# A hybrid encoder layer on one core: stores of transposed queries and keys on another DMA queue, in other slots, and the order of the loads ahead of the first attention head

## The chip, the core and the metric

The kernel runs on one core of a Trainium2 chip. The core has five engines with an instruction stream each: TensorE (PE in the profile; its weight loads are PEld), VectorE (DVE), ScalarE (ACT), GpSimd (POOL) and SyncE (SP). SyncE and ScalarE issue the DMAs of this kernel; in the profile their queues are SPq and ACTq. An engine works through its stream in order, and so does each queue's issuer: an issue that has to wait holds up what stands behind it. The metric is the time of one execution on the device in microseconds. The kernel before took 578.08 us, the median of three runs (575.47 to 578.79).

## What is computed

One layer of an encoder on 1024 tokens of width 1024, with 16 learned tokens ahead of them. The input is normalised once and projected into three groups of mixers: a gated short convolution (256 columns), multi-head attention with compressed queries and keys (8 heads of 64 + 32 features), and a retention mixer (4 heads of 64). The outputs are gated, put side by side and projected back.

```python
u = rms_norm(h, ln_w[l])
(cx, cb, cc, cz, cq, ckv, krope, mz, rq, rk, rv, rz) = jnp.split(u @ w_in[l], IN_OFFSETS, axis=-1)
y_conv = short_conv_mixer(cx, cb, cc, cz, conv_w[l], conv_b[l])
y_mla = mla_mixer(cq, ckv, krope, mz, ...)      # softmax(q k^T) v per head, under a chunk-causal mask
y_ret = retention_mixer(rq, rk, rv, rz, ...)    # intra-chunk scores plus a running state
h = h + jnp.concatenate([y_conv, y_mla, y_ret], axis=-1) @ w_out[l]
```

## The kernel before

Everything is kept in float32. A float32 operand of a matrix product is split into a high part (`h`, rounded by ScalarE) and a low part (`l`, the rest, subtracted by VectorE or GpSimd), and `mm3` (line 114) makes three products of the two pairs. The weights come in tiles of 128 rows by 512 columns (256 KB): SyncE loads one into a staging tile `ws` (three buffers), ScalarE casts its high half and VectorE or GpSimd subtracts its low half (`load_w`, line 117, and `split`, line 102). High and low tiles have 12 buffers each, so the tiles of the next unit of weights can be loaded only as those of the unit before are used up.

The stages follow each other on TensorE: the gates `mz`; the compressed queries and keys `A`, from which `a_up` makes keys and queries of all heads and stores them as `k_s` and `q_s` in DRAM, token by token (lines 392 and 412); the retention mixer in two units `u` of two heads, each over token tiles `t` (`r_proj`, `r_rope`, `r_score`, `r_out`); the convolution in two units and two halves of the tokens `g` (`conv_cx`, `conv_cz`, `conv_cb`, all through `feat`); the attention heads; the output projection `out`. The products of `r_proj` and of `feat` go to a pair of PSUM banks of tag `pj`; ScalarE frees one with `rt` (line 463), VectorE one with the convolution's products (lines 646 to 676).

The attention needs queries and keys with the features on the partitions. This is made beside the retention and convolution stages in eight turns, `turn(i, part)` (line 552): turn `i` treats the keys (`i` even) or the queries (`i` odd) of one pair of heads. Part 0 gathers them from DRAM into `ts` (four loads of 192 KB on SyncE), part 1 transposes them on VectorE into `td` (line 564), part 2 splits them into high halves `th` (ScalarE) and low parts (VectorE, in place in `td`), the queries by single features and with a scale, part 3 stores them in `T_s`, as `kT_s` or `qT_s` (two stores of 384 KB from `th`, one of 768 KB from `td`, lines 582 and 583). `turns()` (line 585) is called once for each token tile of the retention stage and once for each product group of the convolution; each call is a slot. A turn begins in the slot that `BEGIN` names; its part 1 comes two slots later, part 2 three, part 3 four. The tiles `ts` and `td` share two buffers (tag `q`), the halves `th` share two (tag `v`) with the values of the heads, of which `load_pair(0)` (line 686) loads the first behind the convolution's third group (slot 31); the fourth group has slots 32 to 35.

The program is written in this order, but each engine's final order is laid out ahead of the run by a scheduler that simulates the program and gives an engine the earliest written instruction that is ready in the simulation. `tc.issue_after(x)` keeps the instructions in its block that run on the engine of `x` behind `x`; `at["act"]` and `at["dve"]` are the last `rt`, `th` of the gate, or eviction noted. It has no effect on instructions of other engines.

Ahead of the attention, `load_wo` (line 689) loads a tile of output weights (256 KB, SyncE) and returns the splitting of it as a function, `cut`; `load_head(h)` (line 615) loads keys and queries of a head, six loads of 128 KB into `kt` and three of 256 KB into `qt`; `y_split` (line 844) loads finished outputs `y_s` of the other mixers for the `partial` products (line 853), which are spread over the attention as filling. `score(h, t)` (line 748) makes one tile of scores `S`, their maximum and exponentials.

Of the kernel before, what the change touches and what calls it, by code (L numbers as in the profile page):

```python
# [7 lines left out]
F32 = mybir.dt.float32  # L8
# [42 lines left out]
def trunk(tc, ins, outs):  # L51
    from contextlib import ExitStack

    nc = tc.nc
# [27 lines left out]
    T_s = [dp.tile([4, 2, P, 6, 256], F32, name=f"{c}T_s") for c in "qk"]  # L82
# [11 lines left out]
    r = cp.tile([P, 9], F32, name="r")  # L94
# [7 lines left out]
    def split(hi, lo, src, scale=None, lo_eng=None):  # L102

        if scale is None:
            nc.scalar.copy(hi, src)
            (lo_eng or nc.vector).tensor_tensor(lo, src, hi.bitcast(F32), op=ALU.subtract)
        else:
            nc.scalar.activation(hi, src, AF.Copy, scale=scale)
            nc.vector.scalar_tensor_tensor(lo, src, scale, hi.bitcast(F32), op0=ALU.mult, op1=ALU.subtract)
# [63 lines left out]
    with tc.tile_pool(name="ps0", bufs=1, space=PSUM, reuse_waits="tile") as ps0:  # L173
# [96 lines left out]
        for b in range(4):  # L270
# [3 lines left out]
            for g in range(2):  # L274
                i = 2 * b + g
# [47 lines left out]
    act = [None]  # L323
# [122 lines left out]
    oz, at = {}, {}  # L446
# [100 lines left out]
        later(fin)  # L547

    turned, slot = {}, [0]
    BEGIN = (2, 5, 8, 11, 17, 20, 23, 26)  # L550

    def turn(i, part):

        hp, which = i // 2, 1 - i % 2
        if part == 0:
            src = hp_pool.tile([P, NT, 192], F32, tag="q", name=f"ts{i}")
            x = (q_s, k_s)[which].rearrange("t p c -> (t p) c")[:, hp * 192:hp * 192 + 192]
            for j, y in enumerate(x.rearrange("(j n r) c -> j r n c", j=4, r=32)):
                nc.sync.dma_start(src[32 * j:32 * j + 32], y)
            turned[i] = [src]  # L560
        elif part == 1:
            dst = hp_pool.tile([P, 6, 256], F32, tag="q", name=f"td{i}")
            for j in range(2):
                nc.vector.transpose(dst[:, 3 * j:3 * j + 3].rearrange("p c (n k) -> p n c k", k=32),
                                    turned[i][0][:, :, 96 * j:96 * j + 96].rearrange("p n (c k) -> p n c k", k=32))
            turned[i] = [dst]
        elif part == 2:
            dst = turned[i][0]
            for j in range(2):
                hi = hp_pool.tile([P, 3, 256], F32R, tag="v", name=f"th{i}_{j}")  # L570
                x = dst[:, 3 * j:3 * j + 3]
                if which:
                    split(hi, x.bitcast(F32R), x)
                else:

                    for c in range(3):
                        split(hi[:, c], x[:, c].bitcast(F32R), x[:, c], scale=wqk[:, c:c + 1] if c < 2 else None)
                turned[i].append(hi)
        else:
            dst, *hi = turned.pop(i)  # L580
            for j in range(2):
                nc.sync.dma_start(T_s[which][hp, 0, :, 3 * j:3 * j + 3], hi[j].bitcast(F32))
            nc.sync.dma_start(T_s[which][hp, 1], dst)

    def turns():

        n = slot[0]
        slot[0] += 1
        for ago, part in ((4, 3), (3, 2), (2, 1), (0, 0)):
            if n - ago in BEGIN:  # L590
                with tc.issue_after(at["act" if part == 2 else "dve"]):
                    turn(BEGIN.index(n - ago), part)

    for u in range(2):
        for t in [8] + list(range(NT)):
            r_proj(u, t)
            step()
            if t != 8:
                turns()
            if t == 3:  # L600
                if u == 0:
                    wr.append([load_w("r1", k) for k in range(KT)])
                else:
                    wc = [[load_w("c0", k) for k in range(KT)]]


    def feat(u, b, lo_, n, name):
        pp = pst("pj", name)
        for k in range(KT):
            mm3(pp[:, :n], [w[:, b * P:b * P + P] for w in wc[u][k]], X(k, lo_, n), k == 0, k == KT - 1)  # L610
        step()
        turns()
        return pp

    def load_head(h):
        for which in (1, 0):

            src = T_s[which][h // 2].rearrange("s (i f) c r -> c f (s i) r", i=4)
            x = ((qT, kT)[which][h % 2])[:, :, NM * which:NM * which + SEQ].bitcast(F32)
            for c in range(3):  # L620
                cs, y = slice(32 * c, 32 * c + 32), src[3 * (h % 2) + c]
                if which:
                    for s in range(2):
                        nc.sync.dma_start(x[cs, s].rearrange("p (i r) -> p i r", i=4), y[:, 4 * s:4 * s + 4])
                else:
                    nc.sync.dma_start(x[cs].rearrange("p s (i r) -> p (s i) r", i=4), y)
        for i, m_ in enumerate((kmh, kml)):
            nc.gpsimd.tensor_copy(kT[h % 2][:96, i, :NM], m_[:, h].bitcast(F32))

# [59 lines left out]
    def load_wo(k, g):  # L689
        wh = wp.tile([P, 512], F32R, tag="wh", name=f"woh{k}_{g}")  # L690
        wl = wp.tile([P, 512], F32R, tag="wl", name=f"wol{k}_{g}")
        st = at1.tile([P, 512], F32, tag="wst", name=f"wos{k}_{g}", bufs=4)
        nc.sync.dma_start(st, wout_d[:, k, g * 512:g * 512 + 512])
        wo[k, g] = (wh, wl)

        def cut():
            split(wh, wl, st, scale=vec[:, V_RN:V_RN + 1] if k >= 6 else None, lo_eng=nc.gpsimd if g == 0 else nc.vector)
        return cut
# [46 lines left out]
    if True:  # L745
# [98 lines left out]
        def y_split(t):  # L844
            src = wsp.tile([P, 512], F32, tag="ws", name=f"ysrc{t}")
            nc.sync.dma_start(src.rearrange("p (k q) -> p k q", k=4), y_s.rearrange("k p q -> p k q")[:, :, t * P:t * P + P])
            return lambda: y_cut(t, src)
# [16 lines left out]
        seq = [(h, t) for h in range(H) for t in range(NT)]  # L864


    cuts = [load_wo(k, 0) for k in (0, 1, 6, 7)]
    load_head(0)
    ycuts = [y_split(t) for t in range(2)]
    load_head(1)  # L870
    conv_cx(1, 1, 1)
    conv_cx(1, 1, 0)
# [27 lines left out]
    for n in range(len(seq) + 1):  # L900
        if n + LA < len(seq):
            score(*seq[n + LA])
        if n < len(seq):
            h, t = seq[n]
            p_t(h, t)
            turns()
            if t == 0 and h in (0, 2, 4):
                pairs.append(load_pair(h // 2 + 1))
                nc.sync.dma_start(ym[h // 2 + 1], mz_s[h // 2 + 1])

            if t == QK and h + 2 < H:
                load_head(h + 2)
        if 1 <= n and seq[n - 1][1] % 4 == 3:
            attend(seq[n - 1][0], seq[n - 1][1] // 4)
        if n < len(seq):
            h, t = seq[n]
# [146 lines left out]
```

## Time and profile before

| | |
|---|---|
| median of the runs | 578.08 us (575.47 to 578.79, three runs) |
| the profiled execution | 578.73 us, its span 576.6 us |
| TensorE busy | 565.5 us (98%) |
| VectorE, ScalarE, GpSimd busy | 357.9, 253.8, 212.3 us |
| mean granted TensorE clock | 0.993 of full speed |
| SyncE's queue, ScalarE's queue | 84.39 MB, 6.29 MB |

The span goes from the first to the last instruction of one execution. The granted clock is given as a share of 2.4 GHz, 0.5 being 1.2 GHz. In the views below, a wait is put down to the instruction whose end came last before it; a DMA share of 1 or more in a stretch means that the 16 DMA engines had no free time.

### The profile page before, as it was taken

The page shows a single profiled execution, that of the slowest core. Times are in us where ns is not written, and L with a number is a line of the kernel's source. Part 1 is how long each engine was busy: PE and PEld are TensorE (multiplying, and loading weights), DVE is VectorE, ACT ScalarE, POOL GpSimd, SP SyncE. Part 2 cuts the span into 40 slices and gives each one's busy share as a digit, 9 for nine tenths or more (in the row PEclk, how much of TensorE's full clock was granted, in tenths as well). Part 3 has the DMA queues.
Part 4 walks back from the last instruction along what each step waited for, and adds up shares of the span by engine and source line. Part 5 has one row for each costly group of instructions (what it writes and reads, how often), then busy time and mean ns, then how long its engine had stood idle before and what let it go on. Part 6 is the DMA issues. An engine that isn't in the chain of part 4 may idle for free.

```text
span 576.6 us, 9524 instructions
## 1 busy us (share of the span) xinstructions
PE 565.5 (98%) x3294; PEld 474.7 (82%) x3294; DVE 357.9 (62%) x782; ACT 253.8 (44%) x598; POOL 212.3 (37%) x314
## 2 busy tenths in 40 slices
PE   9999999999999999989999989999999999999997
PEld 5888999988887888888889878788788888877886
DVE  6958569887456654767375535766656755766132
ACT  7923465683244424534132114655545644654000
POOL 2123357767113140242231836454524424540000
PEclk9999999999999999989999989999999999999999
DMA  8563325374133634366557698845645637123086
GB/s 325 164 197 126 130 91 175 148 225 152 70 105 134 175 110 152 79 233 202 164 171 236 154 207 274 206 107 151 165 131 143 174 101 203 40 75 107 0 300 229
DMA packets 61567, 91.28 MB, mean 158 GB/s; under 512 B 5424, under 2 KB 35760, under 8 KB 61392
## 3 DMA queue, kind: packets, MB, share of 16 engines
q1 hardware_dynamic: 57920, 84.39, 49.4%
q10 hardware_dynamic: 3600, 6.29, 3.0%
q8 instruction: 26, 0.43, 0.3%
q14 instruction: 21, 0.17, 0.1%
HBM read 57.07 MB, written 33.59 MB: 157 GB/s over the span
## 4 chain that ended last, share of the span: by engine, by line
PE 85%; DVE 5%; DMA 4%; ACT 2%; issue 1%; POOL 1%; SPq 1%; DVEq 0%; POOLq 0%; ACTq 0%
PE r L114 13%; PE S L114 9%; PE mz L114 8%; PE out L114 8%; PE part L114 8%; PE A L114 7%; PE o L832 6%; PE pTp L791 5%; PE cv L114 5%; PE qps L114 3%; PE cz L114 3%; PE cb L114 2%; DMA ws_c<-in_win 2%; DMA ysrc<-y_s 1%; PE kps L114 1%
## 5 line engine op out<-in xcount | busy, mean ns | idle before, releaser
L114 PE MATMUL S<-kt,qt 104*128 104x144 f32 (+6 forms) x336 | 65.6, 328 | 1.6 <-DMA ysrc<-y_s 1.6
L769 ACT ACTIVATE pr<-S,smx 128x144 f32<-128x144 f32 (+8 forms) x72 | 50.3, 699 | 36.3 <-DVE smx L760 22.2
L760 DVE TENSOR_REDUCE smx<-S 128x1 f32<-128x144 f32 (+8 forms) x72 | 50.8, 705 | 20.7 <-PE S L114 9.3
L114 PEld LDWEIGHTS S<-kt,qt 104*128 104x128 f32 x336 | 54.9, 190 | 7.7 <-issue 2.3
L777 POOL TENSOR_SCALAR pm<-pr,smx 128x16 f32<-128x16 f32 x64 | 19.5, 304 | 85.8 <-DVE smx L775 80.8
L797 ACT COPY pt<-pTp 128x512 f32<-128x512 f32 (+2 forms) x64 | 32.2, 504 | 38.9 <-PE pTp L791 38.8
L778 POOL TENSOR_SCALAR pr<-pr,smx 128x128 f32<-128x128 f32 (+3 forms) x64 | 47.7, 746 | 0.0
L791 PE MATMUL pTp<-ident,pr 128*128 128x128 f32 x288 | 45.6, 277 | 1.3 <-DVE pt L795 0.9
L791 PEld LDWEIGHTS pTp<-ident,pr 128*128 128x128 f32 x288 | 34.2, 140 | 9.8 <-issue 3.7
L476 POOL TENSOR_SCALAR kw<-qk,con 128x64 f32<-128x64 f32 (+1 forms) x36 | 15.1, 433 | 70.2 <-DVE qk L472 58.6
L832 PE MATMUL o<-pt,v 128*64 128x256 f32 (+2 forms) x448 | 39.4, 311 | 0.0
L832 PEld LDWEIGHTS o<-pt,v 128*64 128x64 f32 x448 | 27.3, 136 | 11.2 <-issue 4.2
L114 PE MATMUL r<-wh_r,xah 128*128 128x512 f32 (+1 forms) x80 | 30.6, 382 | 0.0
L114 PE MATMUL r<-wl_r,xah 128*128 128x512 f32 (+1 forms) x80 | 30.2, 378 | 0.0
L951 DVE SCALAR_TENSOR_TENSOR ot<-out,xr 128x512 f32<-128x512 f32 (+1 forms) x17 | 11.2, 661 | 30.5 <-PE out L114 17.2
L114 PE MATMUL r<-wh_r,xal 128*128 128x512 f32 (+1 forms) x80 | 29.9, 373 | 0.0
L114 PE MATMUL part<-woh,yh 128*128 128x512 f32 x64 | 29.6, 463 | 0.0
L114 PE MATMUL r<-wl_r,xbh 128*128 128x512 f32 x64 | 26.0, 406 | 0.0
L114 PE MATMUL r<-wh_r,xbl 128*128 128x512 f32 x64 | 25.6, 400 | 0.0
L114 PE MATMUL r<-wh_r,xbh 128*128 128x512 f32 x64 | 25.6, 400 | 0.0
L114 PE MATMUL part<-wol,yh 128*128 128x512 f32 x64 | 25.3, 395 | 0.0
L114 PE MATMUL part<-woh,yl 128*128 128x512 f32 x64 | 25.1, 393 | 0.0
(276 smaller groups left out, 1558.0 us busy)
## 6 DMA issues: line engine op xcount, KB each, us to landing
kt<-kT_s SPq DMA_DIRECT2D x48, 128.0 KB, 4.2
qt<-qT_s SPq DMA_DIRECT2D x24, 256.0 KB, 5.8
ws_r<-in_win SPq DMA_DIRECT2D x16, 256.0 KB, 3.0
ws_c<-in_win SPq DMA_DIRECT2D x16, 256.0 KB, 3.5
wos<-in_wout SPq DMA_DIRECT2D x16, 256.0 KB, 4.1
xp<-in_x SPq DMA_DIRECT2D x16, 256.0 KB, 5.1
p_s<-xp SPq DMA_DIRECT2D x16, 256.0 KB, 2.2
xr<-p_s SPq DMA_DIRECT2D x15, 256.0 KB, 4.0
```

The source lines that it names most:

```text
L114: m = nc.tensor.matmul(out, lhsT=x_, rhs=y_, start=first and i == 0, stop=last and i == 2)
L476: nc.gpsimd.tensor_scalar(kw[R, j], qk[R, 2 + j], con[R, kd0 + j:kd0 + j + 1], 1.0, op0=ALU.mult, op1=ALU.mult)
L760: at["dve"] = nc.vector.tensor_reduce(sm[:, i // 2:i // 2 + 1], sp[:, :n, :w], axis=AX.XY, op=ALU.max, negate=True).ins
L769: e = nc.scalar.activation(pr[:, c0:c1].rearrange("p (b c) -> p b c", b=n), sp, AF.Exp, bias=mx, accum_out=sm[:, 5 + i:6 + i])
L777: nc.gpsimd.tensor_scalar(pm[(2 * h + t // 4) % 2][:, t % 4, :NM], pr[:, nk - NM:nk], sm[:, 9:10], 1.0, op0=ALU.mult, op1=ALU.mult)
L778: nc.gpsimd.tensor_scalar(pr[:, :nk - NM], pr[:, :nk - NM], sm[:, 9:10], 1.0, op0=ALU.mult, op1=ALU.mult)
L791: tr_ = nc.tensor.transpose(out=tp[:, b * P:b * P + P], in_=pr[:, c0:c0 + P], identity=ident)
L797: nc.scalar.copy(pt[:, b0:b0 + nb, tt], src)
L832: nc.tensor.matmul(op[64 * cg:64 * cg + 64, c0:c1], lhsT=lv, rhs=src[:, i_, c_], start=b == 0, stop=False)
L951: nc.vector.scalar_tensor_tensor(ot, acc[:, c0:c1], 0.5, xt, op0=ALU.mult, op1=ALU.add)
```

## The change

The stores of part 3 are issued from ScalarE's stream and not from SyncE's, and `issue_after` now holds them behind the last noted ScalarE instruction. The eight turns begin in other slots: turns 0 and 1 two slots earlier, 2 and 3 where they were, 4 and 5 one slot earlier, 6 and 7 three slots later. The loads of head 0 are written ahead of the four loads of output weights, and the three loads of its queries are issued from ScalarE's stream.

```diff
-    BEGIN = (2, 5, 8, 11, 17, 20, 23, 26)
+    BEGIN = (0, 3, 8, 11, 16, 19, 26, 29)
...
             for j in range(2):
-                nc.sync.dma_start(T_s[which][hp, 0, :, 3 * j:3 * j + 3], hi[j].bitcast(F32))
-            nc.sync.dma_start(T_s[which][hp, 1], dst)
+                nc.scalar.dma_start(T_s[which][hp, 0, :, 3 * j:3 * j + 3], hi[j].bitcast(F32))
+            nc.scalar.dma_start(T_s[which][hp, 1], dst)
...
-                with tc.issue_after(at["act" if part == 2 else "dve"]):
+                with tc.issue_after(at["act" if part >= 2 else "dve"]):
...
-    def load_head(h):
+    def load_head(h, eng=None):
...
-                    nc.sync.dma_start(x[cs].rearrange("p s (i r) -> p (s i) r", i=4), y)
+                    (eng or nc.sync).dma_start(x[cs].rearrange("p s (i r) -> p (s i) r", i=4), y)
...
+    load_head(0, nc.scalar)
     cuts = [load_wo(k, 0) for k in (0, 1, 6, 7)]
-    load_head(0)
     ycuts = [y_split(t) for t in range(2)]
```

## Rows read from the trace of the kernel before

**Rows 1.** The page's first part: busy us (share of span) and instructions by engine.

```profile
PE 565.5 (98%) x3294; PEld 474.7 (82%) x3294; DVE 357.9 (62%) x782; ACT 253.8 (44%) x598; POOL 212.3 (37%) x314
```

**Rows 2.** Waits of TensorE: who waited for whom, total us, times, longest.

```profile
PE cv L114 <- ACT rt L463: 2.3, 1, 2.3
PE S L114 <- DMA ysrc<-y_s: 1.6, 1, 1.6
...
PE rtp L481 <- DVE state L514: 1.0, 1, 1.0
```

**Rows 3.** Busy us by stretch: start:end, length, engines, granted clock, DMA share, GB/s.

```profile
185.00:188.00 3.00, 1.98 (x16) 1.50 (x15) 2.47 (x7) 2.82 (x7) 0.00 (x0) 1.00 0.50 141
240.00:245.00 5.00, 5.00 (x34) 4.58 (x34) 4.92 (x14) 4.73 (x14) 0.64 (x2) 1.00 1.09 221
245.00:250.00 5.00, 2.70 (x21) 2.44 (x20) 3.66 (x10) 2.74 (x6) 2.08 (x2) 1.00 0.92 354
247.40:249.70 2.30, 0.01 (x1) 0.01 (x1) 1.57 (x3) 2.12 (x5) 0.90 (x1) 1.00 1.05 427
250.00:255.00 5.00, 5.00 (x32) 5.00 (x31) 3.03 (x8) 0.86 (x3) 3.91 (x4) 0.66 0.55 214
331.00:336.50 5.50, 5.50 (x24) 4.10 (x22) 1.98 (x3) 0.53 (x1) 0.00 (x0) 1.00 1.14 209
336.50:338.10 1.60, 0.05 (x2) 0.07 (x1) 0.00 (x0) 0.00 (x0) 0.00 (x0) 1.00 1.18 231
340.00:345.00 5.00, 5.00 (x18) 4.06 (x18) 3.42 (x5) 2.07 (x5) 3.46 (x3) 0.68 1.04 206
```

**Rows 4.** Issues of SyncE's queue in order of time: start us, us, what.

```profile
238.89 0.81 SPq L559 DMA_DIRECT2D ts<-k_s  x2
...
240.75 0.92 SPq L559 DMA_DIRECT2D ts<-k_s  x2
241.77 0.87 SPq L121 DMA_DIRECT2D ws_c<-in_win  x2
242.73 1.42 SPq L582 DMA_DIRECT2D qT_s<-th  x2
```

**Rows 5.** ScalarE in order of time near 248 (idle before, releaser).

```profile
247.44 1.32 ACT L105 CAST wh_c<-ws_c 128x512 fp32r<-128x512 f32 x2 [2.10 <-DMA ws_c<-in_win]
...
248.95 0.69 ACT L463 ACTIVATE rt<-r,r 128x512 f32<-128x512 f32 x1
```

**Rows 6.** Issues of SyncE's queue ahead of the first scores.

```profile
322.35 2.19 SPq L693 DMA_DIRECT2D wos<-in_wout  x4
324.64 2.75 SPq L624 DMA_DIRECT2D kt<-kT_s  x6
329.02 2.52 SPq L626 DMA_DIRECT2D qt<-qT_s  x3
331.64 0.95 SPq L846 DMA_DIRECT2D ysrc<-y_s  x2
```

**Rows 7.** ScalarE in order of time behind the first scores.

```profile
339.64 0.62 ACT L105 CAST yh<-ysrc 128x512 fp32r<-128x512 f32 x1 [8.10 <-DMA ysrc<-y_s]
...
344.27 0.38 ACT L769 ACTIVATE pr<-S,smx 128x144 f32<-128x144 f32 x1 [2.15 <-DVE smx L760]
```

**Rows 8.** VectorE in order of time, five rows between 170 and 201.

```profile
170.49 0.95 DVE L106 TENSOR_TENSOR td<-td,th 128x768 fp32r<-128x768 f32 x1
...
184.14 0.69 DVE L106 TENSOR_TENSOR wl_r<-ws_r,wh_r 128x512 fp32r<-128x512 f32 x1 [2.21 <-ACT wh_r L105]
...
189.69 1.82 DVE L564 STREAM_TRANSPOSE td<-ts 128x768 f32<-128x768 f32 x2
...
199.94 0.88 DVE L109 SCALAR_TENSOR_TENSOR td<-td,wqk,th 128x256 fp32r<-128x256 f32 x2
200.73 0.42 DVE L106 TENSOR_TENSOR td<-td,th 128x256 fp32r<-128x256 f32 x1
```

**Rows 9.** Issues of line 952 on ScalarE's queue: ns min/median/max, first and last start.

```profile
L952 ACTq DMA_DIRECT2D out<-ot x17: 338/360/362, 546.9 to 573.7; - x17
```

## The prediction

> **What bounds the kernel now.** I read the page's engine table first: TensorE is busy for 565.5 of 576.6 us [rows 1], so a change that removes no matrix work can only win where TensorE stands still or runs at its lower clock. The waits of TensorE say where it stands: 2.3 us in the feature products `cv`, 1.6 us in the first scores `S`, 1.0 us in a transpose of the retention stage [rows 2]. The busy times by stretch then give the place and the clock [rows 3]. The stop in `cv` is 247.40 to 249.70; in the 5 us behind it the granted clock is 0.66, that is, part of the time at 1.2 instead of 2.4 GHz, which costs 0.34 x 5 = 1.7 us more. The stop in `S` is 336.50 to 338.10 with 0.05 us of work in it (1.55 us lost); behind it the clock is 0.68 from 340 to 345, and 0.32 x 5 = 1.6 us are lost. The stop of 1.02 us inside 185 to 188 has a clock of 1.00 and costs itself alone. I call these stops B (2.3 + 1.7 = 4.0 us), C (1.55 + 1.6 = 3.15 us) and A (1.0 us). All three together, 8.2 us, are the most that an edit of queues can give.
>
> Each has its cause in the queues. **C:** SyncE issues four loads of output weights from 322.35, then the six key loads of head 0 from 324.64, then its three query loads from 329.02 to 331.54, then `ysrc` [rows 6]; the DMA engines' share is 1.14 to 1.18 while they move 209 to 231 GB/s [rows 3], so they are full, and the first score waits until the queries, last in line, have landed. **B:** TensorE needs a PSUM bank that ScalarE frees with `rt`; `rt` runs at 248.95 because the cast before it stood 2.10 us for a weight tile [rows 5] that SyncE issued in the pair from 241.77, behind the gathers of the next turn (`ts`) and just ahead of the stores `qT_s` of the turn before [rows 4]. **A:** VectorE's `state` update is late [rows 2]; in front of it stands the block of subtractions for the weights of `r1`, of which the last runs at 184.14 [rows 8].
>
> **The change part by part.** (1) *Head 0's loads ahead of the output weights, its queries on ScalarE's queue.* The four weight loads are 4 x 256 KB = 1 MB; at the 209 GB/s of rows 3 they hold the engines for 5.0 us ahead of keys and queries. Issuing the queries beside the keys also takes away their turn in SyncE's line: 329.02 - 322.35 = 6.7 us lie between the first of the four weight issues and the first query issue [rows 6], and some of the 6.7 us is the same 5.0 us. So the queries should land at least 5 us sooner, at about 333 instead of 338, and C needs only 1.55: C goes, clock loss included, **-3.15 us**; bounds 0 and -3.15. What is late next are the weights and `ysrc`. ScalarE's copy of `ysrc` already waits 8.10 us until 339.64, and the first exponential follows it at 344.27 [rows 7]. The weights are used only in the `partial` products behind the first heads' scores, and I cost their delay at nothing because `ysrc`, the other operand of these products, is behind them already; without that cover the price is again 1 MB, 5.0 us.
>
> (2) *Stores on ScalarE's queue.* Eight turns with three stores, and three query loads: 27 issues. One issue on ScalarE's queue takes 0.36 us [rows 9], so 27 x 0.36 = 9.7 us go onto an engine that is busy for 44% [rows 1], at most 1.1 us in one place. They now stand behind the slot's `rt`, in order: behind them wait the next `tanh`, copies and casts, and for these wait PSUM banks and weights. I take nothing for it, because the two halves of `pj` give TensorE one whole product to go on with; the upper bound is in the third rival. On the other side stop B gains. By position the two weight loads of 241.77 are ahead of the stores of 242.73, so at first sight the stores cost them nothing. The bytes say a little more: from 240 to 247.44 the engines moved 5 x 221 + 2.44 x 354 = 1969 KB [rows 3], while four gathers of 192 KB and three weight loads of 256 KB are 1536 KB. So 433 KB, mostly of the stores, went through before the weights were complete, and at 354 GB/s that is 1.2 us. In the changed kernel these stores come behind `rt` of the last retention slot. Bounds: 0 (order in the queue) and -4.0 (all of B and its clock). I take the bytes, **-1.2 us**, and leave the clock's 1.7 us where it is: a stop of 1.1 us is left, near A's 1.02 with a clock of 1.00 and not far from C's 1.55 with a slow one.
>
> (3) *Other slots.* Turns 0 and 1 begin two slots earlier. In the DVE block ahead of A, turn 0's two subtractions of 0.95 us leave (1.9 us). Turn 1 arrives: two transposes, 1.82 us together, and its split, which on the query side is 0.88 + 0.42 us for each half, 2.6 us [rows 8]. Net 1.82 + 2.6 - 1.9 = +2.5 us on VectorE. Right ahead of the last subtraction VectorE idles for 2.21 us [rows 8], so between 0.3 and 2.5 us can reach A; with a slow clock behind it (1.7 us, as at B) the upper bound is +4.2, and the lower one, if the earlier turn 0 unties the block, is -1.0. I take **+0.8**, nearer to the idle time than to none of it. Turns 4 and 5 move by one slot beside `cv`, with evictions between them: nothing, since in rows 4 the gathers follow the freeing of a buffer and not the slot. Turns 6 and 7 move three slots later, turn 7 into the stretch in which head 0 is loaded, which matters for the third rival.
>
> Sum: -3.15 - 1.2 + 0.8 = -3.55 us. The profiled execution took 578.73 us (span 576.6, 2.1 around it), so 575.2; the median of the three runs, 578.08, is 0.65 lower, and there the sum gives **574.5 us**, -0.6%. A measurement of this kernel can tell about 0.5%, 2.9 us, from no change, so this is just beyond that line.
>
> **Rivals.** *First, B goes altogether*: the stop of 1.1 us left goes as well, and with it the clock's 1.7 us, another -2.8: 571.7 us. For it: C's and B's slow clocks follow stops of 1.55 and 2.3, A's 1.02 has none. Against: the weights are issued ahead of the stores already.
>
> *Second, the next wait takes C's place.* If the copy of `ysrc` stays ahead of the exponentials on ScalarE, it still ends the wait near 339.64, since keys, queries, 1 MB of weights and `ysrc` are the same bytes on engines that are full; TensorE would come 3.15 us sooner to transposes whose probabilities aren't there. All of C is given back: -1.2 + 0.8 = -0.4, 577.7 us. For it speaks rows 7, against it that the exponentials' scores come sooner and need not queue behind it. The Trainium skill (DMA: Bandwidth & Descriptors, "Issuing engines are not separate DMA queues") speaks for this rival: transfers started by ScalarE and SyncE run on the same 16 engines, and a second issuer saves only issue time. The full engines of rows 3 agree with it.
>
> *Third, slower: turn 7 collides with head 0.* Its three stores, 1.5 MB, now fall where the engines are full, on the same queue as the queries. Its two halves also share one buffer of tag `v`, the other being held by `load_pair(0)`, so they go one behind the other. If they get ahead of the queries, then 1.5 MB and 0.75 MB of queries on ScalarE's queue run beside as much on SyncE's: 4.5 MB from 322.35 at 220 GB/s (between 209 and 231) end at 342.8 instead of 338.1. C grows by 4.7 instead of going: -1.2 + 0.8 + 4.7 = +4.3, 582.4 us. It decides when the queries land later than 338.1. Against it: the queries need only free buffers to go, and turn 7 has a gather, transposes and casts to do first.
>
> *Fourth, A takes the full 4.2*: 3.4 more, 577.9 us.
>
> **How the numbers follow.** Forecast 0.40 (its own range 573 to 576.5, three quarters of it faster by over 0.5%, that is under 575.2); first rival 0.15, second 0.20, third 0.15, fourth 0.10. Faster: 0.30 + 0.15 = 0.45. Same: 0.10 + 0.20 and most of the fourth, 0.08 = 0.38. Slower: 0.15 + 0.02 = 0.17. The range reaches from the first rival to most of the third: 571.0 to 581.5 us.
>
> **What would show it.** Right: no wait of TensorE before the first `S`, full clock behind it, query issues on ScalarE's queue beside SyncE's key issues, `qT_s` stores behind the `rt` that frees `cv`, and a stop of about 1 us there. Second rival: a new wait of TensorE on `pr` or `part` near 345, behind a copy of `yh` that waits for `ysrc`. Third: `S` waits beyond 338 while stores of `th` are under way. Fourth: `rtp` or `r` waits several us near 186, with a clock below 1. Wrong altogether: if ScalarE's issues wait for landings of earlier transfers, so that `rt` is late in several slots.

## The result and the profile after

The changed kernel takes 571.23 us (four runs, 571.08 to 572.71) beside 577.65 us of the kernel before: a ratio of 0.9897, 95% interval 0.9871 to 0.9923. A second comparison, made later, gave 573.15 us (six runs, 571.23 to 574.26) beside 577.55 us: 0.9916, interval 0.9887 to 0.9945. So it is faster by 4.4 to 6.4 us, where 3.6 were forecast. The profiled execution took 572.71 us, its span is 570.7 us, 5.9 less than before.

First the page's first part, and the waits of TensorE (who waited for whom: total us, times, longest), both of the changed kernel:

```profile
PE 562.3 (99%) x3294; PEld 473.5 (83%) x3294; DVE 356.9 (63%) x782; ACT 254.4 (45%) x598; POOL 214.1 (38%) x314
```

```profile
PE cv L114 <- ACT rt L463: 2.4, 1, 2.4
...
PE pTp L791 <- DVE pt L795: 0.9, 2, 0.6
PE pTp L791 <- POOL pr L778: 0.2, 1, 0.2
```

Beside [rows 2], the waits of `S` and of `rtp` are gone (C and A of the prediction), and the wait of `cv`, B, is as long as it was. The busy times by stretch of the changed kernel (columns as in [rows 3]) say the same of the clock:

```profile
185.00:188.00 3.00, 3.00 (x21) 2.46 (x19) 1.49 (x5) 1.31 (x3) 0.61 (x2) 1.00 0.97 282
240.00:245.00 5.00, 5.00 (x37) 4.61 (x35) 4.96 (x17) 4.18 (x12) 0.70 (x2) 1.00 1.05 242
245.00:250.00 5.00, 2.57 (x16) 2.32 (x15) 3.52 (x10) 2.40 (x5) 2.02 (x1) 0.86 0.62 175
250.00:255.00 5.00, 5.00 (x36) 5.00 (x36) 2.91 (x6) 0.79 (x2) 3.12 (x4) 0.80 0.77 311
340.00:345.00 5.00, 5.00 (x31) 4.50 (x30) 2.69 (x6) 1.59 (x6) 5.00 (x10) 1.00 1.14 228
```

TensorE is busy throughout 185 to 188 and 340 to 345, at full clock. Behind the stop in `cv` the clock falls as it did, now over two stretches: 0.14 x 5 + 0.20 x 5 = 1.7 us. When TensorE reaches its stages (the view by tile: first start, and for `out` the start of the last product, in us):

| | `r` | `cv` | `cz` | `part` | last of `out` |
|---|---|---|---|---|---|
| before | 117.7 | 243.2 | 261.0 | 350.3 | 572.9 |
| after | 118.0 | 242.1 | 260.0 | 345.0 | 567.0 |
| gained in the stage that ends there | -0.3 | 1.4 | -0.1 | 4.3 | 0.6 |

Now the queues, SyncE first, around the stop in `cv` and ahead of the first scores (start us, us, what):

```profile
239.63 0.94 SPq L559 DMA_DIRECT2D ts<-k_s  x2
240.67 0.86 SPq L121 DMA_DIRECT2D ws_c<-in_win  x2
245.70 3.16 SPq L121 DMA_DIRECT2D ws_c<-in_win  x3
...
321.17 4.62 SPq L624 DMA_DIRECT2D kt<-kT_s  x6
325.84 3.71 SPq L693 DMA_DIRECT2D wos<-in_wout  x4
329.59 3.42 SPq L846 DMA_DIRECT2D ysrc<-y_s  x2
```

And ScalarE in the same two places (idle before and its releaser in brackets; ACTq are the DMA issues in its stream):

```profile
246.46 1.32 ACT L105 CAST wh_c<-ws_c 128x512 fp32r<-128x512 f32 x2 [2.24 <-DMA ws_c<-in_win]
247.30 0.84 ACTq L582 DMA_DIRECT2D qT_s<-th  x2
...
247.97 0.69 ACT L463 ACTIVATE rt<-r,r 128x512 f32<-128x512 f32 x1
...
318.19 1.54 ACTq L626 DMA_DIRECT2D qt<-qT_s  x3
...
334.80 0.62 ACT L105 CAST yh<-ysrc 128x512 fp32r<-128x512 f32 x1
337.85 0.62 ACT L105 CAST yh<-ysrc 128x512 fp32r<-128x512 f32 x1 [2.43 <-DMA ysrc<-y_s]
338.38 0.38 ACT L769 ACTIVATE pr<-S,smx 128x144 f32<-128x144 f32 x1
```

The queries now go at 318.19, beside the keys and 10.8 us earlier than in [rows 6]; the first copy of `ysrc` runs at 334.80, 4.8 us earlier than in [rows 7], and the first exponential at 338.38, 5.9 us earlier. Around 247 nothing has changed but the place of the stores: the cast still stands 2.24 us for a weight tile (2.10 in [rows 5]), although the stores `qT_s` are now issued only behind it, at 247.30. That is still ahead of the `rt` at 247.97, and not behind it as the prediction's sign had it. The last query was issued at 331.09 before and landed 6.8 us later, just ahead of the first `S`; now the last query lands at 324.5 and the last key at 329.6, and `S` starts at 332.2.

### The profile page after: what moved, and what is told of

It reads as the page before. It is cut to its first block, busy times and chain, and to the rows that moved or that the text cites. A ratio compares the mean times of both kernels' runs of the same rounds, so it can differ in the third digit from the quotient of the medians.

```text
span 570.7 us, 9518 instructions
## 1 busy us (share of the span) xinstructions
PE 562.3 (99%) x3294; PEld 473.5 (83%) x3294; DVE 356.9 (63%) x782; ACT 254.4 (45%) x598; POOL 214.1 (38%) x314
## 4 chain that ended last, share of the span: by engine, by line
PE 95%; DVE 2%; DMA 1%; ACT 1%; issue 1%; SPq 0%; POOL 0%; ACTq 0%; DVEq 0%; POOLq 0%
PE r L114 15%; PE S L114 9%; PE mz L114 8%; PE out L114 8%; PE part L114 8%; PE cv L114 8%; PE A L114 7%; PE o L832 6%; PE pTp L791 5%; PE cz L114 4%; PE cb L114 4%; PE qps L114 3%; PE kps L114 1%; PE vps L114 1%; PE rsp L502 1%; DMA ws_c<-in_win 1%
```

## The experiments

All ratios are to the kernel before, run beside them, with 95% intervals. Three kernels do one part of the change alone, five take a part out of it, two test a cause of B that the trace of after suggested, and two are repeated. Where a kernel is priced against the changed kernel, the ratio of the changed kernel is taken as the mean of its two, 0.9907; with the intervals of both sides, such a price is uncertain by about 2 us.

**The first head alone** (kernel before, plus):

```diff
+    load_head(0, nc.scalar)
     cuts = [load_wo(k, 0) for k in (0, 1, 6, 7)]
-    load_head(0)
```

> The kernel before with one part of the change: the first head's loads go ahead of the output weights', and its queries are issued by ScalarE. Stores and turns stay. Theory (the gain in front of the first S comes from this part alone; the stop in rtp goes with the stores): the wait of S (1.55 us) goes with its clock, the S, pTp and part landmarks come 3.0 to 4.0 us earlier relative to the end of the c1 wave, and the whole is 573.5 to 574.8 us beside 577.7; the 1.02 us stop in rtp and the 2.3 us stop in cv stay. Rival (ysrc and yh are merely the next thing to be waited for, the store of y and the loads behind it being what is late): S waits for nothing but the chain into pr ends as late as before, within 0.5 us of 577.7. Rival (the stores' departure from SyncE's queue is what let the head come early): this kernel gains at most 1 us.

Measured: 575.69 us, ratio 0.9947 (0.9926 to 0.9968), that is 3.1 us. The waits of TensorE in this kernel:

```profile
PE cv L114 <- ACT rt L463: 3.5, 1, 3.5
...
PE rtp L481 <- DVE state L514: 1.1, 1, 1.1
```

The wait of `S` is gone, those of `cv` and `rtp` are not, and from 310 to 350 us the granted clock is 1.00 where it was 0.96. The gain is that of C in the prediction, 3.15 us, with an interval of 1.8 to 4.3 us. Both rivals fall: the chain into `pr` comes earlier too (336.65 instead of 344.27), and the stores need not leave SyncE's queue for it. The absolute range was 0.9 us too low.

**The stores alone** (kernel before; lines 582 and 583 on `nc.scalar`, and `part >= 2` in `turns()`).

> The kernel before with one part of the change: the stores of turned queries and keys are issued by ScalarE (and their edge, from part 2 on, hangs on ScalarE). Head loads and turns stay. Theory: state stands ahead of the first split of the c0 weights in VectorE's order, as in the changed kernel, so the 1.02 us stop in rtp goes with its clock: -1.0 to -1.6 us; the cv stop of 2.3 us stays, since ScalarE's casts of c1 weights still stand ahead of the last retention wave's rt; the S stop stays: 576.1 to 576.7 us. Rival by the prediction's reading (the stores' bytes and places ahead of ws_c make the cv stop): cv's stop falls to under 0.5 us, first cv comes 2 to 4 us earlier, 573.5 to 575.5 us.

Measured: 576.47 us, ratio 0.9976 (0.9954 to 0.9998), 1.4 us. The stop in `rtp` is gone, that in `cv` is 2.6 us. VectorE in order of time shows why; first this kernel, then the kernel before behind the row at 184.14 of [rows 8]:

```profile
183.82 0.69 DVE L106 TENSOR_TENSOR wl_r<-ws_r,wh_r 128x512 fp32r<-128x512 f32 x1 [1.28 <-ACT wh_r L105]
184.43 0.57 DVE L514 SCALAR_TENSOR_TENSOR state<-state,con,rup 64x64 f32<-64x64 f32 x2
...
185.78 0.69 DVE L106 TENSOR_TENSOR wl_c<-ws_c,wh_c 128x512 fp32r<-128x512 f32 x1
```

```profile
185.49 0.69 DVE L106 TENSOR_TENSOR wl_c<-ws_c,wh_c 128x512 fp32r<-128x512 f32 x1 [0.65 <-ACT wh_c L105]
186.09 0.57 DVE L514 SCALAR_TENSOR_TENSOR state<-state,con,rup 64x64 f32<-64x64 f32 x2
```

In the kernel before, one subtraction for a tile of the *next* unit of weights (`wl_c`) stood in VectorE's order ahead of `state`, and waited 0.65 us for the cast of its tile. The scheduler's new order puts it behind. The rival that the prediction's reading of B stood for, a `cv` stop under 0.5 us, falls.

**The slots alone** (kernel before, with the changed `BEGIN`).

> The kernel before with one part of the change: the turns' places (0, 3, 8, 11, 16, 19, 26, 29 for 2, 5, 8, 11, 17, 20, 23, 26). Theory: both stops (rtp 1.0, cv 2.3) stay and so does S's; turns 0 and 1 two slots earlier and 6 and 7 three later lie beside other work: 577.2 to 578.2 us. Rival (the order of VectorE that frees rtp comes from turn 0 and 1's places, not from the stores): rtp's stop goes, 576.1 to 576.7. Rival (turn 7 three slots later makes its stores late for the first head's loads, which in this kernel stand behind them on SyncE): S waits 1 to 4 us longer, 578.7 to 582.

Measured: 576.08 us, ratio 0.9963 (0.9938 to 0.9989), 2.1 us where the theory had none. The waits of TensorE:

```profile
PE cv L114 <- ACT rt L463: 2.7, 1, 2.7
...
PE S L114 <- DMA qt<-qT_s: 0.8, 1, 0.8
...
PE r L114 <- ACT rt L463: 0.4, 1, 0.4
```

The second expectation holds: the stop in `rtp` goes by the slots alone too. From 256 to 310 us TensorE is busy for 54.00 of 54 us (53.73 before): the short wait of `cv` for VectorE in the convolution, 0.3 us before, is gone as well. The third expectation, a longer wait of `S`, falls: it is 0.8 instead of 1.6.

**The change without the first head's part.**

> The changed kernel without the first head's part: stores and turns as changed, the head's loads behind the output weights on SyncE. Theory (parts add up): the stop in rtp is gone, the cv stop of 2.4 stays, S waits as before or longer by up to 1 us since turn 7 ends later: 575.5 to 577 us, so 4 to 5.5 us above the changed kernel. Rival (the stores off SyncE already bring the head's loads forward): S does not wait, under 573 us.

Measured: 578.03 us (574.35 to 582.29), ratio 1.0002 (0.9968 to 1.0037): no gain at all, where the two parts alone give 1.4 + 2.1 = 3.5 us. Neither expected range holds. The convolution ends as early as in the changed kernel (the last product of `cb` starts at 342.8 in both, at 347.8 before); the loss stands right behind it. TensorE's waits, and ScalarE there:

```profile
PE part L114 <- DVE xp L861: 1.4, 1, 1.4
PE S L114 <- ACT pr L769: 1.2, 2, 0.7
...
PE pTp L791 <- POOL pr L778: 0.6, 2, 0.3
```

```profile
339.38 0.62 ACT L105 CAST yh<-ysrc 128x512 fp32r<-128x512 f32 x1 [5.73 <-DMA ysrc<-y_s]
...
343.42 0.38 ACT L769 ACTIVATE pr<-S,smx 128x144 f32<-128x144 f32 x1 [1.89 <-DVE smx L760]
```

TensorE is there 5.0 us earlier, but `ysrc`, the first exponential and `xp` come hardly earlier than before: the last product of `out` starts at 571.9, only 1.0 us ahead. This is the prediction's second rival, in a kernel that loads the head late.

**The casts of the c1 weights behind the last `rt`** (changed kernel, plus):

```diff
+    rt_last = at["act"]
...
-            wc.append([load_w("c1", k) for k in range(KT)])
+            with tc.issue_after(rt_last):
+                wc.append([load_w("c1", k) for k in range(KT)])
```

The trace of after shows that the tiles whose casts hold `rt` at 246.46 belong to the convolution's second unit of weights, `c1`, which TensorE first uses at 296.8 us. `issue_after` holds only their ScalarE casts, not their loads.

> The changed kernel with one line more: the casts of the c1 weights are queued on ScalarE behind the last retention wave's rt (an edge from that rt on the load of the c1 weights), so that a weight that lands late no longer holds rt. Theory (the stop in cv is ScalarE standing at a cast whose ws_c has not landed, with rt behind it): the 2.4 us stop goes or falls below 0.5 us, and with it the stretch of lower granted clock at 245 to 255 us: first part, o and out come 2.4 to 4 us earlier, 567.2 to 569.5 us beside the changed kernel's 571.2. Rival (rt would come no sooner, because r itself or VectorE's side is just as late): the stop stays at 1.5 to 2.5 us under another name, 570.5 to 571.5. Rival (the c1 casts now come late for c1, a new stop at the first cz): 571 to 573.

Measured: 569.67 us (569.55 to 570.48), ratio 0.9871 (0.9853 to 0.9889). ScalarE around the place, and the busy times by stretch:

```profile
244.88 0.69 ACT L463 ACTIVATE rt<-r,r 128x512 f32<-128x512 f32 x1
...
246.70 1.28 ACT L105 CAST wh_c<-ws_c 128x512 fp32r<-128x512 f32 x2 [0.62 <-DMA ws_c<-in_win]
```

```profile
245.00:250.00 5.00, 4.99 (x42) 4.80 (x40) 4.82 (x14) 2.13 (x4) 3.57 (x2) 1.00 1.03 351
250.00:255.00 5.00, 4.70 (x39) 4.70 (x40) 3.57 (x5) 2.81 (x6) 4.10 (x5) 1.00 0.50 163
```

`rt` runs 3.1 us earlier, the stop of 2.4 us is down to 0.3, and the clock is 1.00. The first `part` comes at 341.8 instead of 345.0. The weights are as late as ever (the cast waits until 246.70); they only hold nothing now. The time is 0.2 us above the range of the theory, and its mechanism is what the trace shows.

> The changed kernel with the c1 casts behind the last retention wave's rt, a second time, since the changed kernel itself came out at 0.9897 and 0.9916 of the kernel before in two comparisons whose intervals overlap with that of this one (0.9871). Theory (the stop in cv is gone for good and with it the granted clock's fall at 250 to 255 us): 569.5 to 570.5 us, ratio 0.986 to 0.988, no stop in cv over 0.5 us, granted clock 1.00 from 236 to 256 us. Rival (the first comparison was lucky with the clock): 571 to 573 us, a clock below 0.95 somewhere in 236 to 350 us.

Measured on another chip: 569.39 us (569.03 to 570.33), ratio 0.9857 (0.9831 to 0.9882). No stop in `cv` over 0.4 us, clock 1.00 from 236 to 256. The nine runs of this kernel and the ten of the changed kernel don't overlap (569.0 to 570.5, and 571.1 to 574.3), so this version beats both kernels, though the runs are from several chips.

**The same line in the kernel before.**

> The kernel before with one line more and nothing of the change: the casts of the c1 weights are queued behind the last retention wave's rt on ScalarE. Theory (the order on ScalarE makes the stop in cv, whoever stores where): the 2.3 us stop goes or falls below 0.5 us, the 1.0 us stop in rtp and S's 1.6 us wait stay; 575 to 576.3 us beside 577.6. Rival (in the kernel before the stores that SyncE queues around the c1 weights make a stop of their own): at least 1 us of the cv stop stays, 576.5 to 577.6 us.

Measured: 575.56 us, ratio 0.9960 (0.9937 to 0.9982), 2.3 us. The waits of TensorE:

```profile
PE S L114 <- DMA ysrc<-y_s: 1.7, 1, 1.7
PE rtp L481 <- DVE state L514: 1.3, 1, 1.3
...
PE cv L114 <- DVE ccs L648: 1.0, 1, 1.0
...
PE cv L114 <- ACT wh_c L105: 0.5, 1, 0.5
```

The wait for `rt` is gone without any store moved; C and A stay. In its place 1.0 us stands in `cv` at 251, for a product of VectorE, so the rival, that at least 1 us of the stop stays, is half right. The 0.5 us for `wh_c` stand at 298, where `c1` begins: its casts are now late there. The first `cz` comes 2.6 us earlier than before; 1.3 us of that are the shorter wait, and in the profiled execution the clock stays at 1.00. So the order on ScalarE makes the wait for `rt`, in both kernels, but in the kernel before a second wait stands close behind it.

**The queries on SyncE** (changed kernel; `load_head(0)` still ahead of the weights, without `nc.scalar`).

> The changed kernel, but the first head's queries are issued by SyncE (still ahead of the output weights). Theory (order counts, not the engine that issues: nine issues of some 0.6 us each on SyncE, keys 4.6 us in the profile of the changed kernel): the queries go 4 to 5 us later, but S at 332 us had no wait and the keys end at 326: at most 0.5 us is lost, 571 to 572. Rival (taking the queries off SyncE is what makes ysrc and yh early): ysrc is issued 1.5 to 3 us later, yh with it, pr and pTp come 1 to 3 us later: 572 to 574.

Measured: 574.76 us, ratio 0.9948 (0.9923 to 0.9972), 2.4 us behind the changed kernel (uncertain by 1.8), so the theory falls and its rival holds, though the time is above the rival's range. SyncE's issues in this kernel:

```profile
319.04 3.34 SPq L624 DMA_DIRECT2D kt<-kT_s  x6
322.53 1.69 SPq L626 DMA_DIRECT2D qt<-qT_s  x3
324.57 6.24 SPq L693 DMA_DIRECT2D wos<-in_wout  x4
330.86 0.98 SPq L846 DMA_DIRECT2D ysrc<-y_s  x2
```

The convolution is 1.7 us earlier here than in the profiled execution of the changed kernel (the last product of `cz` starts at 334.5 and 336.2, no clock lost), yet the first of the two `ysrc` loads is issued 1.3 us later, 3.0 us in all; the second is issued earlier (331.39 and 332.63) but lands later, 7.3 us behind its issue instead of 5.1. Besides the queries' 1.69 us, the four weight loads take 6.24 us from the first to the last issue instead of 3.71; 3.70 us of this are a pause behind the first of them. TensorE then waits 0.8 us in `S` and 0.8 us in `pTp` for the probabilities. The Trainium skill (DMA: Bandwidth & Descriptors, "Issuing engines are not separate DMA queues") says that a second issuer saves only the time of issuing, usually small beside the transfer. One issue is small here too, 0.30 to 0.34 us beside the 4.0 to 5.3 us in which such a load landed in the changed kernel. The price, 2.4 us, lies in what SyncE issues behind the three; how much of it is the pause and the later landing is not shown.

**The weights first** (changed kernel; `load_wo` ahead of `load_head(0, nc.scalar)`).

> The changed kernel, but the output weights are loaded ahead of the first head's keys and queries (queries still issued by ScalarE). Theory (order counts): keys and ysrc go 1.5 to 3 us later than in the changed kernel, the first S comes behind the end of cz as before and the time is 572.5 to 575 us. Rival (only the queries' queue counts): no difference from the changed kernel, 571 to 571.7.

Measured: 574.64 us (572.04 to 578.52), ratio 0.9966 (0.9936 to 0.9996), 3.4 us behind the changed kernel, in the theory's range. Its profile is of the shortest of the six runs. There the first `S` comes at 336.2, behind the last `cz` as the theory had it, and the keys go at 323.42, 2.3 us later than in the changed kernel, but `ysrc` goes earlier, at 327.79; 0.5 us of waiting for `pr` in `S` are all the waiting that it adds. Where the other runs lose more isn't shown.

**Turns 6 and 7 in their old slots** (changed kernel; `BEGIN` ends in 23, 26).

> The changed kernel with turns 6 and 7 back at 23 and 26 (26 and 29 in the change). Theory of the prediction (later slots cost nothing and give nothing while the stores land ahead of the first head's queries): within 0.5 us of the changed kernel, 570.7 to 571.7. Rival (the later slots take the turns out of VectorE's way in the c1 wave, which is where the changed kernel has 0.6 us that the sum does not explain): 572 to 573.5. Rival (the later slots collide with the first head's loads, and the earlier ones set them free): 569.5 to 570.7.

Measured: 574.70 us, ratio 0.9938 (0.9910 to 0.9965), 1.8 us behind the changed kernel, which is within the uncertainty of such a price; the time is above the ranges of all three expectations. The first rival's mechanism is in the trace. Waits of TensorE in the convolution that the changed kernel doesn't have:

```profile
PE cv L114 <- DVE ccs L646: 0.4, 1, 0.4
PE cv L114 <- DVE yv L676: 0.3, 1, 0.3
```

VectorE is busy for 32.81 us from 256 to 310 us, in the changed kernel for 27.99: turn work beside the convolution holds the evictions that free its PSUM banks. The later slots move it to a stretch where no wait of TensorE is put down to it.

**The stores back on SyncE** (changed kernel otherwise).

> The changed kernel with the stores of turned queries and keys back on SyncE; head and turns as changed. Theory (the stores' queue matters because turn 7's last stores stand on SyncE ahead of or between the first head's loads, as 339.9 to 341.8 us in the kernel with the turns alone): keys or ysrc come later, S or pTp 1 to 3 us later, 572.5 to 574.5 us. Rival (with the head first and the turns moved the stores' queue is worth nothing): within 0.7 us of the changed kernel, 570.7 to 571.9 us.

Measured: 574.97 us, ratio 0.9950 (0.9922 to 0.9978), 2.5 us behind. The theory's cause isn't in the trace: no store stands among the first head's loads, whose keys go at 322.49, and the next stores go at 340.22. `S` starts without waiting for queries, but then waits 1.6 us for `pr`; and there is a stop of the kind of B in the retention stage, in `r` for `rt`, 1.2 us. ScalarE ahead of it:

```profile
189.42 1.30 ACT L105 CAST wh_c<-ws_c 128x512 fp32r<-128x512 f32 x2
193.21 0.62 ACT L105 CAST wh_c<-ws_c 128x512 fp32r<-128x512 f32 x1 [2.50 <-DMA ws_c<-in_win]
193.85 0.47 ACT L463 ACTIVATE rt<-r,r 16x256 f32<-16x256 f32 x1
```

Four casts of the unit `c0` stand ahead of an `rt` here; in the changed kernel `rt` stands behind the second and runs at 190.61.

**The changed kernel again.**

> The changed kernel itself beside these two on one chip, for its spread and a second profile. If its gain is what its ten or so microseconds of removed waits make, 571 to 572 us with a spread of about 2 us. If the stop in cv brings the clock's fall with it, the second profile shows a granted clock under 0.95 in the windows behind the stop, at 250 to 255 us; if the fall is not tied to the stop, the stop of 2.2 to 2.6 us is there at a clock of 1.00, as in the kernels with the queries on SyncE and with the output weights first.

Measured: 573.15 us, as told above, beyond the 571 to 572 us expected; the runs spread over 3.0 us. The stop in `cv` is 2.5 us, and the clock falls behind it:

```profile
245.00:250.00 5.00, 2.52 (x20) 2.26 (x19) 3.48 (x10) 2.40 (x5) 2.02 (x1) 1.00 0.63 185
250.00:255.00 5.00, 5.00 (x32) 5.00 (x31) 2.90 (x6) 0.79 (x2) 3.43 (x4) 0.66 0.81 320
```

With the queries on SyncE or the weights first the same stop (2.2 and 2.4 us) was there at 1.00. So the fall can follow the stop and need not.

## Why the prediction was partly right

The direction was right, and the forecast 2.5 us short on the profiled executions (3.55 worked out, 6.0 measured); the first comparison's time lies 0.2 us inside the lower end of the range, the second's 2.2 us. Of the forecast's own range, 573 to 576.5, the first time lies below and the second just inside. The two smaller terms were wrong, one in sign, and a part costed at nothing seems to have given something. Their errors go opposite ways, B's term promising too much and A's too little, so that the sum is no farther off is in part luck.

**C, -3.15 us: right, in size and mechanism.** The first head alone gives 3.1 us; queries ahead, no wait of `S`, full clock behind it. What I costed at nothing stayed there: no `part` waits for weights, and no wait of TensorE is put down to the issues in ScalarE's stream. The cover I named, `ysrc`, held. The second rival, which would have given C back, did not come because `ysrc` itself came 2.0 us earlier on SyncE's queue and its first copy 4.8 us earlier; with the head left out, it did come and took the gains of the other two parts with it. The third did not: no query waits for turn 7's stores. They overlap, since the queries are issued at 318.19 and the last store of `td` at 326.82, and the loads land early enough.

**B, -1.2 us: wrong, it was 0.** The step that failed is the one from bytes to the landing of the weights. With the stores out of the way the cast waits 2.24 us instead of 2.10. The load that it waits for takes no less, 5.8 us from its issue to the cast (240.67 to 246.46) and 5.7 before (241.77 to 247.44). The busy times of the wait (columns as in [rows 3]), first in the changed kernel, then in the kernel before:

```profile
243.60:246.46 2.86, 2.68 (x21) 2.43 (x20) 2.07 (x6) 0.62 (x1) 1.65 (x3) 1.00 0.58 175
```

```profile
244.70:247.44 2.74, 2.69 (x21) 2.43 (x20) 2.09 (x6) 0.62 (x2) 1.52 (x3) 1.00 0.85 265
```

Without the stores' bytes the engines only move less, at a share of 0.58, and the weights come no sooner: the stores' bytes had gone through beside the weights and had not held them up. What does hold the weights is not shown. The bytes were also counted too high: 354 GB/s is the mean up to 250, and up to 247.44 it was 284, which leaves 264 KB over instead of 433. Besides, I asked only when the tile lands and not who needs it: [rows 5] shows the cast in front of `rt`, and the tile was for a unit that starts some 50 us later. The runs with the c1 casts behind `rt` show that cause: the wait for `rt` goes in both kernels, with the weights as late as ever, for 2.3 us in the kernel before and about 2 to 3 us in the changed one. The first rival (B goes altogether, 571.7) has nearly the measured time, and is still wrong: B stayed whole.

**A, +0.8 us: wrong sign, it was -1.0, and -1.4 with the rest of its stage.** I took the stop for one of load on VectorE and counted its work; the work did grow, from 7.37 to 9.42 us between 174 and 186 us, and TensorE waited for none of it. The stop came from the order: `wl_c`, waiting for a late tile, stood ahead of `state`. The last subtraction that I quoted, at 184.14, is not the last one; `wl_c` at 185.49 is the one in front of `state`. Either the stores or the slots alone are enough for the scheduler to lay out another order. That this order came out better is not a property of either part: with head and slots but the stores on SyncE, another stop of 1.2 us took its place. The fourth rival, A at 4.2, was never near.

**Turns 6 and 7, costed at nothing: probably wrong.** They give 1.8 us by the ratios (0.9938 against 0.9907), uncertain by 1.9; 0.7 us are seen in the trace, as waits for VectorE's evictions, and how the rest comes about is not shown. The wait of 0.3 us for `yv` stood in the trace of before, too short for me to look into.

**What stays open.** Of the 5.9 us in the span, A's stop accounts for 1.0, C with its clock for 3.15 and the wait for `yv` for 0.3; 1.4 us, spread over the stages, have no line of their own. And the single parts add up (3.1 + 1.4 + 2.1 = 6.6), while pairs don't: head and slots together lose 2.5 us against the whole, stores and slots all of it. Head and stores without the slots were not run.

## What to carry to other kernels

When an engine frees a buffer late, look at what stands ahead of the freeing instruction in its fixed order, and ask when that is needed: a cast for weights used 50 us later cost a stop that the moved stores did not cure, and one line did. A change to queues under a scheduler is also a change to every engine's order, so compare the orders before pricing bytes. And a gain in front of a stage can be lost if the stage's own loads don't come forward with it, as it was here without the first head's part.

## What the runs showed of the hardware

The granted clock falls behind a stop of 2.2 to 2.5 us in some executions and not in others, so its price is a matter of frequency. The mean clock of a run was below 0.998 in 58 of the 79 runs of the kernel before that stood beside the experiments, in 9 of 10 with the first head alone (where the stop in `cv` is left), in 5 of 10 of the changed kernel, in 2 of 10 of the kernel before with the c1 casts behind `rt`, and in none of the 9 of the changed kernel with it. A fall to 0.997 is 0.003 x 577 = 1.7 us, the same as the 0.34 x 5 us of one stretch at 0.66.

A block of issues on SyncE can take much longer while the 16 engines are full: four loads of 256 KB took 2.19 us from first to last issue in [rows 6], at a DMA share of 0.61, 3.71 us in the changed kernel at 1.07, and 6.24 us with the queries on the same queue at 1.10. In the last, the first issue takes 1.24 us, and then SyncE issues nothing for 3.70 us, from 325.81 to 329.51; what it waits for is not shown.
